# Moving a 64-byte offset from the low parts to the high parts of split weights

## The chip, the cores and the metric

The kernel runs on one core of one Trainium2 chip, in one launch. The metric is the device time of that launch in microseconds. The engines named below are TensorE (PE in the profile, its weight loads PEld), VectorE (DVE), ScalarE (ACT), GpSimd (POOL) and the sync engine (SP), which issues most of the DMAs.

## The reference

The reference is one decoder layer over 256 tokens and a model width of 2048, all in float32:

```python
proj = x @ w_in                      # 13,336 columns: gq gk gv gr glr fq fk fv ff ma mb
y_gla = (rms(gla(q, k, v, log_a)) * g * silu(gr)) @ w_branch_gla
y_fox = fox_attention(fq, fk, fv, log_f) @ w_branch_fox
x = layer_norm(ALPHA * x + (sigmoid(ma) * y_gla + sigmoid(mb) * y_fox) @ w_out)
h = gelu(causal_dwconv(x @ w_gate, conv_w, conv_b)) * (x @ w_up)     # width 5632
x = layer_norm(ALPHA * x + h @ w_down)
x = x + sigmoid(x @ w_ple_gate) * (p @ w_ple_proj)
```

Nearly all of the work is the products of the 256 rows of `x` with some 400 MB of weights.

## The kernel before, in words

**Split products.** A float32 product is made of three products of the type float32r, which the kernel uses as a shorter float32. Each operand is split into a high part (`hi`, a copy into float32r, on ACT) and a low part (`lo = raw - hi`, on DVE). The product is then high by high, high by low and low by high. An activation tile (`xT`, `x1T`, `x2T`) holds, for each of its four blocks of 128 rows of the contraction, 256 high columns (the tokens) and after them 256 low columns.

**Units.** The weights are cut into 284 units of 128 partitions by 2048 columns, in the order in which they are used. `prep()` prepares the next unit: two DMAs fill two tiles `raw` (1024 columns each), ACT writes the two tiles `hi`, DVE the two tiles `lo`. `prep_s()` does the same for units that are multiplied by Strassen's scheme, with the inner function `split()`. `unit()` keeps about three units ahead. The tiles `hi` come from the pool `rhi` and the tiles `lo` from the pool `rlo`, six buffers each, which are used in turn. In `rhi` a buffer has 1024 columns of 4 bytes (4,096 bytes in each partition), in `rlo` 1152 columns (4,608 bytes), of which 1024 are used. Both steps are multiples of 512 bytes.

**Two ways to multiply.** The units 32 to 135 and 224 to 283 (`UA`) have moving weights: 128 columns of an activation are loaded into TensorE, and 512 columns of `hi` or `lo` stream past (`x_mm`, `q_unit`, `s_half`; the tiles `psm`, `psa`, `psb`, `gv`, `gr`, `wo`, `dn`, `pg`). The units 0 to 31 (the queries and keys of both mixers) and 136 to 223 (gate and up projection) have stationary weights: 128 columns of the weights are loaded, and the activations stream past. `w_unit` issues 16 pairs of matmuls for each of these units, into the tiles `psfq`, `psfk`, `psq`, `psk`, `psg` and `psu`. The first of a pair (L307, called the long one below) has 128 columns of `hi` as its stationary operand and streams 512 columns, the high and the low half of the activation. The second (L309, the short one) has 128 columns of `lo` and streams the 256 high columns alone. The first three units of the gate and up stage are multiplied in two phases by `w_phase`: there the `hi` matmuls (L322) stream 256 columns too, half of the tokens, as do the `lo` matmuls (L326).

**Offsets.** `lo_tile(u, name)` gives the tile for a low part. For a unit of `UA` the low part begins at the start of its buffer; for a unit with stationary weights it begins `LO_SHIFT` = 16 columns, 64 bytes, into it. High parts begin at the start of their buffers everywhere.

**Order.** SP's queue and parts of PE's are written out by hand; elsewhere the order is that of the program, moved by priorities. A weight load (LDWEIGHTS) is made by the compiler for each matmul.

Of the kernel before, what the change touches and what calls it, by code (L numbers as in the profile page):

```python
# [10 lines left out]
F32R = mybir.dt.float32r  # L11
# [8 lines left out]
P = 128  # L20
# [15 lines left out]
GAPS = (96, 64, 80)  # L36


LO_SHIFT = 16
UA = (range(32, 136), range(224, 284))  # L40
P_STAT = 5000
P_LN1 = (4000, 2000)
# [36 lines left out]
def tile_block(ctx: ExitStack, tc: tile.TileContext, wu, wfv, wpp, xT_in, x_in, pT_in, wlr,  # L79
# [11 lines left out]
    rhi = ctx.enter_context(tc.tile_pool(name="rhi", bufs=6))  # L91
    rlo = ctx.enter_context(tc.tile_pool(name="rlo", bufs=6))
# [12 lines left out]
    def s8(shape, dt=F32, name=None):  # L105
        return big.tile(shape, dt, tag="S8", name=name)

    def t1(name):
        return sm.tile([P, 256], F32, tag="t1", bufs=6, name=name)
# [10 lines left out]
    def copy(o, i, scale=1.0):  # L120
        return nc.scalar.activation(o, i, AF.Copy, bias=0.0, scale=scale)  # L121
# [29 lines left out]
    hS = {}  # L151

    def lo_tile(u, name):
        o = 0 if any(u in r for r in UA) else LO_SHIFT
        return rlo.tile([P, 1152], F32R, tag="lo", name=f"lo{name}")[:, o:o + 1024]

    def differences(r0, r1, h, pinned=False):
        b12, b11, b22, b21 = r0[:, 0:512], r0[:, 512:1024], r1[:, 0:512], r1[:, 512:1024]
        sub = lambda o, a, b: nc.vector.tensor_tensor(o, a, b, ALU.subtract)  # L159
        if h == 0:  # L160
            i = sub(b11, b12, b11)
            if pinned:
                tc.keep_in_program_order(i)
            sub(b12, b12, b22)
        else:
            sub(b22, b22, b11)
            sub(b21, b21, b22)
# [17 lines left out]
    def prep_s(u):  # L185


        r0, r1 = [ring.tile([P, 1024], F32, tag="raw", bufs=5, name=f"raw{u}_{h}")
                  for h in range(2)]
        b12, b11, b22, b21 = r0[:, 0:512], r0[:, 512:1024], r1[:, 0:512], r1[:, 512:1024]  # L190
        rt = (r0, r1)
        if u in parked:
            nc.sync.dma_start(b11, wu[u, :, 512:1024])
            nc.sync.dma_start(r1, wu[u, :, 1024:2048])
            w = s8([P, 2048], name=f"td{u}")
            nc.sync.dma_start(w, td[parked[u]])
            rt = (w[:, 0:1024], w[:, 1024:2048])
        else:
            for h, r in enumerate((r0, r1)):
                nc.sync.dma_start(r, wu[u, :, h * 1024:(h + 1) * 1024])  # L200
        if dn0 <= u < dn0 + NF:
            nh = (u - dn0) // (NF // 2)
            pair = DN_ORDER[nh][(u - dn0) % (NF // 2)]
            i = DN_S[0].index(pair)
            if i % 2 == 0:
                two = s8([P, 8, 256], F32R, name=f"hS{nh}_{pair}")
                nc.sync.dma_start(two.bitcast(F32), sd[i // 2].rearrange(
                    "p (i n) -> p i n", i=8))
                hS[nh, pair], hS[nh, DN_S[0][i + 1]] = two[:, 0:4], two[:, 4:8]

        def split(src, name, e=slice(0, 1024)):
            hi = rhi.tile([P, 1024], F32R, tag="hi", name=f"hi{u}_{name}")[:, e]
            lo = lo_tile(u, f"{u}_{name}")[:, e]
            copy(hi, src)
            nc.vector.tensor_tensor(lo, src, hi.bitcast(F32), ALU.subtract)  # L215
            return [(hi[:, o:o + 512], lo[:, o:o + 512]) for o in range(0, src.shape[1], 512)]

        x11, = split(b11, "b11", slice(512, 1024))
        x22, x21 = split(r1, "b2")
        if u not in parked:  # L220
            differences(r0, r1, 0)
        t3, t1_ = split(rt[0], "t13")
        if u not in parked:
            differences(r0, r1, 1)
        t2_, t4 = split(rt[1], "t24")
        ready[u] = [x11, x21, x22, t1_, t3, t2_, t4]

    def prep(pinned=False):
        u = n_prep[0]
        n_prep[0] += 1  # L230
        if u in s_units:
            prep_s(u)
            return
        his, los = [], []
        for h in range(2):
            raw = ring.tile([P, 1024], F32, tag="raw", bufs=5, name=f"raw{u}_{h}")
            nc.sync.dma_start(raw, wu[u, :, h * 1024:(h + 1) * 1024])
            hi = rhi.tile([P, 1024], F32R, tag="hi", name=f"hi{u}_{h}")
            copy(hi, raw)
            lo = lo_tile(u, f"{u}_{h}")  # L240
            i = nc.vector.tensor_tensor(lo, raw, hi.bitcast(F32), ALU.subtract)  # L241
            if pinned:
                tc.keep_in_program_order(i)
            his.append(hi)
            los.append(lo)
        ready[u] = (his, los)


    def unit(ahead=3):
        u = n_used[0]  # L250
        n_used[0] += 1
        while n_prep[0] < min(NU, u + ahead):
            prep()
        return ready.pop(u)
# [203 lines left out]
    for u in range(8):  # L458
        hi, lo = fvu[u]
        for j in range(2):  # L460
# [8 lines left out]
            for t, i, c in seq:  # L469
                o, n = fch[c]  # L470
# [14 lines left out]
        elif u == 4:  # L485
            load_consts()
    prep()
    prep()
    wraw = s8([GROWS, 1024], name="wraw")
    nc.gpsimd.memset(wraw, 0.0)  # L490
# [161 lines left out]
    for n in range(16):  # L652
        h, j = n // 2, n % 2
        hi, lo = unit()
# [114 lines left out]
    for n in range(16):  # L769
        nm, dst, sc = (("q", gq, 1.0 / 16.0), ("k", gk, 1.0))[n // 2 % 2]  # L770
        h, c = n // 4, n % 2
        hi, lo = unit()
# [647 lines left out]
    for n in range(NF):  # L1420
# [18 lines left out]
        u = t1("up")  # L1439
# [4 lines left out]
        if pair in DN_S[0]:  # L1444
            if j == 0:
                yp = t2("yp").rearrange("p (k t) -> p k t", t=S)
            h = yp[:, j, :]
        else:
            h = y
# [4 lines left out]
        if pair in DN_S[0] and j == 1:  # L1454
            v = s_sums(yp)
            for i in range(2):
# [5 lines left out]
                o = k % 2 * 1024 + 512 * i  # L1462
# [295 lines left out]
```

## Time and profile before

| | |
|---|---|
| median of 3 runs | 1645.13 us (1644.68 to 1645.78) |
| the profiled execution | span 1645.0 us from the first to the last instruction |
| TensorE | 1638.4 us, 8422 matmuls; weight loads 1404.3 us |
| VectorE, ScalarE, GpSimd | 1356.0 us, 910.3 us, 92.7 us |
| granted TensorE clock | 1.000 |
| from HBM | 417.53 MB, 290 GB/s over the span |

TensorE has a matmul in work all the time, so a matmul's recorded duration overlaps the next one's. What counts is the distance from one start to the next. The view of the chain of waits merges matmuls that follow each other without a gap, with the time of the whole stretch and their number: a stretch divided by its number is that distance.

### The profile page before, as it was taken

What the parts mean: (1) busy time and instruction counts of PE and PEld (TensorE: products, weight loads), DVE (VectorE), ACT (ScalarE), POOL (GpSimd) and SP (SyncE); (2) the same over time, 40 slices, a digit from 0 to 9 for tenths busy, and PEclk for the clock granted to TensorE, in tenths of its full rate; (3) what the DMA queues carried; (4) which work ended last, traced back from release to release, by engine and by line L of the source; (5) the groups of instructions that cost most, each with busy time, mean ns of one, the idle gap of its engine ahead of it and who ended that gap; (6) DMA issues with size and microseconds to landing.
All of it is one profiled execution on the core that took longest, in us unless ns stands there. A gap on an engine that the chain in (4) does not pass through costs nothing.

```text
span 1645.0 us, 23490 instructions
## 1 busy us (share of the span) xinstructions
PE 1638.4 (100%) x8422; PEld 1404.3 (85%) x8422; DVE 1356.0 (82%) x1964; ACT 910.3 (55%) x1277; POOL 92.7 (6%) x244
## 2 busy tenths in 40 slices
PE   9999999999999999999999999999999999999998
PEld 9988888888888888887898888888888888888887
DVE  7687899788989867778987888887887778988887
ACT  6655555456666654446574445555455456566554
POOL 0000000000000000000010111110111000000000
PEclk9999999999999999999999999999999999999999
DMA  8799799878888768889855898888766679899574
GB/s 324 281 371 341 290 383 356 294 258 309 306 333 307 252 207 303 305 335 364 296 190 194 315 338 320 308 306 304 279 239 217 210 260 336 305 343 348 177 258 157
DMA packets 114838, 477.81 MB, mean 290 GB/s; under 512 B 13032, under 2 KB 14320, under 8 KB 95136
## 3 DMA queue, kind: packets, MB, share of 16 engines
q1 hardware_dynamic: 105216, 417.57, 70.8%
q0 software_dynamic: 9504, 58.73, 8.9%
q8 instruction: 66, 1.08, 0.2%
q14 instruction: 52, 0.43, 0.1%
HBM read 417.53 MB, written 58.73 MB: 290 GB/s over the span
## 4 chain that ended last, share of the span: by engine, by line
PE 97%; DMA 1%; DVE 1%; ACT 0%; issue 0%; POOL 0%; ACTq 0%
PE psm L979 11%; PE dn L841 10%; PE psu L307 10%; PE psg L307 9%; PE psa L979 5%; PE psu L309 5%; PE psg L309 5%; PE dn_p L841 4%; PE gr L841 3%; PE gv L841 3%; PE fv L472 3%; PE pg L353 3%; PE psb L979 3%; PE wo L841 2%; PE gr_p L841 2%; PE gv_p L841 2%
## 5 line engine op out<-in xcount | busy, mean ns | idle before, releaser
L241 DVE TENSOR_TENSOR lo<-raw,hi 128x1024 fp32r<-128x1024 f32 x456 | 551.1, 1220 | 140.7 <-ACT hi L121 139.4
L121 ACT ACTIVATE hi<-raw 128x1024 fp32r<-128x1024 f32 x456 | 476.6, 1057 | 304.2 <-DMA raw<-in_wu_dram 83.7
L307 PE MATMUL psu<-x1T,hi 128*128 128x512 f32 x688 | 240.4, 392 | 0.0
L307 PE MATMUL psg<-x1T,hi 128*128 128x512 f32 x672 | 234.8, 392 | 0.0
L309 PE MATMUL psu<-x1T,lo 128*128 128x256 f32 x688 | 192.3, 280 | 0.0
L309 PE MATMUL psg<-x1T,lo 128*128 128x256 f32 x672 | 187.8, 280 | 0.0
L979 PE MATMUL psm<-hi,xT 128*128 128x512 f32 x512 | 163.0, 392 | 0.0
L307 PEld LDWEIGHTS psu<-x1T,hi 128*128 128x128 f32 x688 | 129.2, 188 | 27.6
L307 PEld LDWEIGHTS psg<-x1T,hi 128*128 128x128 f32 x672 | 126.2, 188 | 27.0
L309 PEld LDWEIGHTS psu<-x1T,lo 128*128 128x128 f32 x688 | 130.6, 190 | 0.0
L121 ACT ACTIVATE hi_b<-raw 128x512 fp32r<-128x512 f32 x112 | 92.9, 841 | 66.8 <-DMA raw<-in_wu_dram 17.9
L309 PEld LDWEIGHTS psg<-x1T,lo 128*128 128x128 f32 x672 | 127.6, 190 | 0.0
L159 DVE TENSOR_TENSOR td<-td 128x512 f32<-128x512 f32 x172 | 117.6, 684 | 0.9
L215 DVE TENSOR_TENSOR lo_b<-raw,hi_b 128x512 fp32r<-128x512 f32 x112 | 104.9, 952 | 15.9 <-ACT hi_b L121 15.6
L979 PEld LDWEIGHTS psm<-hi,xT 128*128 128x128 f32 x512 | 96.2, 188 | 19.6
L215 DVE TENSOR_TENSOR lo_t<-td,hi_t 128x1024 fp32r<-128x1024 f32 x86 | 101.7, 1219 | 12.7 <-ACT hi_t L121 12.0
L121 ACT ACTIVATE hi_t<-td 128x1024 fp32r<-128x1024 f32 x86 | 88.0, 1053 | 28.9 <-DMA td<-td 15.1
L979 PE MATMUL psm<-lo,xT 128*128 128x512 f32 x256 | 99.8, 390 | 0.0
L841 PE MATMUL dn<-hi,hC 128*128 128x512 f32 x352 | 97.8, 389 | 0.0
L979 PE MATMUL psa<-hi,oT 128*128 128x512 f32 x256 | 81.2, 392 | 0.0
L841 PEld LDWEIGHTS dn<-hi,hC 128*128 128x128 f32 x352 | 66.0, 188 | 13.7
L979 PEld LDWEIGHTS psa<-hi,oT 128*128 128x128 f32 x256 | 48.1, 188 | 10.0
(414 smaller groups left out, 3130.8 us busy)
## 6 DMA issues: line engine op xcount, KB each, us to landing
raw<-in_wu_dram SPq DMA_DIRECT2D x525, 512.0 KB, 6.3
td<-in_wu_dram SPq DMA_DIRECT2D x43, 1024.0 KB, 8.8
td<-td POOLq DMA_DIRECT2D x43, 1024.0 KB, 7.7
td<-td SPq DMA_DIRECT2D x43, 1024.0 KB, 8.3
hS<-sd SPq DMA_DIRECT2D x11, 1024.0 KB, 8.8
raw<-in_wu_dram SPq DMA_DIRECT2D x43, 256.0 KB, 7.7
fvraw<-in_wfv_dram SPq DMA_DIRECT2D x13, 524.0 KB, 6.6
sd<-hs POOLq DMA_DIRECT2D x24, 256.0 KB, 5.6
```

What stands on the lines that cost most here:

```text
L121: return nc.scalar.activation(o, i, AF.Copy, bias=0.0, scale=scale)
L159: sub = lambda o, a, b: nc.vector.tensor_tensor(o, a, b, ALU.subtract)
L215: nc.vector.tensor_tensor(lo, src, hi.bitcast(F32), ALU.subtract)
L241: i = nc.vector.tensor_tensor(lo, raw, hi.bitcast(F32), ALU.subtract)
L307: nc.tensor.matmul(ps, lhsT=hi[i // 8 if hoff == 0 else 0][:, w0 % 1024:w0 % 1024 + P], rhs=a[:, kt % 4, :], start=first and i == 0, stop= ...
L309: nc.tensor.matmul(ps[:, 256:512], lhsT=lo[i // 8 if hoff == 0 else 0][:, w0 % 1024:w0 % 1024 + P], rhs=a[:, kt % 4, 0:256], start=False, ...
L353: nc.tensor.matmul(bs[j][:, 0:m], lhsT=x, rhs=v[:, o:o + m], start=first and i == 0, stop=last and i == 2)
L472: nc.tensor.matmul(fbk[t][c][:, 0:n], lhsT=x, rhs=w[:, o:o + n], start=kt == 0 and i == 0, stop=kt == 15 and i == 2)
L841: nc.tensor.matmul(ps[:, e], lhsT=x, rhs=w, start=k == 1, stop=k == total.get(id(ps), 3 * ns))
L979: nc.tensor.matmul(ps[t], lhsT=x, rhs=v, start=first and i == 0 and j == 0, stop=last and i == 3 and j == 2)
```

## The change

In units with stationary weights the high parts now begin 64 bytes into their buffers and the low parts at the start. In units of `UA` both begin at the start, as before. The spare columns go with it: a buffer of `rhi` has 1152 columns now, a buffer of `rlo` 1024. The two pools together keep their size, so all tiles behind them stay where they are. No instruction is added, removed or put in another place.

```diff
-LO_SHIFT = 16
+HI_SHIFT = 16
...
     def lo_tile(u, name):
-        o = 0 if any(u in r for r in UA) else LO_SHIFT
-        return rlo.tile([P, 1152], F32R, tag="lo", name=f"lo{name}")[:, o:o + 1024]
+        return rlo.tile([P, 1024], F32R, tag="lo", name=f"lo{name}")
+
+    def hi_tile(u, name):
+        o = 0 if any(u in r for r in UA) else HI_SHIFT
+        return rhi.tile([P, 1152], F32R, tag="hi", name=f"hi{name}")[:, o:o + 1024]
...
         def split(src, name, e=slice(0, 1024)):
-            hi = rhi.tile([P, 1024], F32R, tag="hi", name=f"hi{u}_{name}")[:, e]
+            hi = hi_tile(u, f"{u}_{name}")[:, e]
             lo = lo_tile(u, f"{u}_{name}")[:, e]
...
-            hi = rhi.tile([P, 1024], F32R, tag="hi", name=f"hi{u}_{h}")
+            hi = hi_tile(u, f"{u}_{h}")
             copy(hi, raw)
             lo = lo_tile(u, f"{u}_{h}")
```

## The prediction

> **What bounds the kernel now.** I read the page first: the busy times, the chain that ended last, then who waited for whom on TensorE.
>
> ```profile
> span 1645.0 us, 23490 instructions
> PE 1638.4 (100%) x8422; PEld 1404.3 (85%) x8422; DVE 1356.0 (82%) x1964; ACT 910.3 (55%) x1277; POOL 92.7 (6%) x244
> PE 97%; DMA 1%; DVE 1%; ACT 0%; issue 0%; POOL 0%; ACTq 0%
> ```
>
> ```profile
> PE warm_ps L131 <- DVE warm L128: 1.2, 1, 1.2
> PE wo L841 <- DVE lo_b L215: 0.4, 1, 0.4
> PE wo_p L841 <- ACT hi_t L121: 0.2, 1, 0.2
> ```
>
> TensorE is the bound from end to end: 97% of the chain is matmuls, and the waits of TensorE for other engines come to 1.8 us, none of them at a unit with stationary weights. What the change can move is therefore the distance between matmuls. The groups of the units with stationary weights come next, which are the only units where an address within 512 bytes changes (columns: busy us, mean ns of one, then the engine's idle us before them).
>
> ```profile
> L307 PE MATMUL psu<-x1T,hi 128*128 128x512 f32 x688 | 240.4, 392 | 0.0
> L307 PE MATMUL psg<-x1T,hi 128*128 128x512 f32 x672 | 234.8, 392 | 0.0
> L309 PE MATMUL psu<-x1T,lo 128*128 128x256 f32 x688 | 192.3, 280 | 0.0
> ...
> L309 PEld LDWEIGHTS psu<-x1T,lo 128*128 128x128 f32 x688 | 130.6, 190 | 0.0
> L307 PEld LDWEIGHTS psu<-x1T,hi 128*128 128x128 f32 x688 | 129.2, 188 | 27.6
> ...
> L309 PE MATMUL psfq<-xT,lo 128*128 128x256 f32 x128 | 35.9, 280 | 0.0
> L309 PE MATMUL psk<-xT,lo 128*128 128x256 f32 x128 | 35.8, 280 | 0.0
> ```
>
> These are 688 pairs for `psu`, 672 for `psg` and four times 128 for the queries and keys (two of the four rows): 1,872 pairs. The loads differ by the part: 188 ns for `hi`, 190 ns for the shifted `lo`. Before a load of `hi` the load port is idle (27.6 us over 688 loads, 40 ns each), before a load of `lo` never. The timeline of a piece of the gate and up stage shows why: matmuls first, then the loads in the same place.
>
> ```profile
> 1000.15 0.28 PE L309 MATMUL psg<-x1T,lo 128*128 128x256 f32 x1
> 1000.27 0.39 PE L307 MATMUL psg<-x1T,hi 128*128 128x512 f32 x1
> 1000.50 0.28 PE L309 MATMUL psg<-x1T,lo 128*128 128x256 f32 x1
> ```
>
> ```profile
> 1000.16 0.19 PEld L307 LDWEIGHTS psg<-x1T,hi 128*128 128x128 f32 x1
> 1000.27 0.19 PEld L309 LDWEIGHTS psg<-x1T,lo 128*128 128x128 f32 x1
> ```
>
> A load starts with the matmul ahead of its own. So `hi` is loaded under a short matmul: load at 1000.16, its matmul already at 1000.27, about 0.07 us before the recorded end of the load (the record has that much of a tail). And `lo` is loaded under a long matmul: load at 1000.27, its matmul at 1000.50, 0.04 us after the end of the load. The load under the long matmul has about 110 ns to spare, the load under the short one none that shows here. The change exchanges which of them is the shifted one. The chain of waits gives the distances without rounding.
>
> ```profile
> 900.25 0.23 PE psg L307
> ...
> 904.41 0.23 PE psg L307
> ```
>
> ```profile
> 627.02 10.88 PE psb L979 x48
> ...
> 542.84 2.09 PE go L1084 x9
> ...
> 834.26 1.44 PE psg L322 x12
> ...
> 1638.07 1.20 PE pg_11c L909 x10
> ```
>
> Twelve pairs lie between the first two rows: 4.16 us, 346.7 ns for a pair. Matmuls of 512 columns with an unshifted load under each (`psb`, moving weights) stand 10.88/48 = 226.7 ns apart, those of 256 columns (`psg` at L322, `pg_11c`) 1.44/12 = 1.20/10 = 120.0 ns. The sum of the two is 346.7 ns. So a pair costs today just what its matmuls cost alone with unshifted loads: the shift of `lo`, under the long matmul, costs nothing. `go` is a chain of 512 columns that is slower: 2.09/9 = 232.2 ns, 5.5 ns more for each, without an idle moment. Its operands are no weights: `vh` and `vl` come from a pool that lies behind tiles of a few bytes each, so most of its streams start at another place within 512 bytes. I take it for the size of what an address can cost.
>
> **The change part by part.** *Units with moving weights.* The new buffers stand 4,608 bytes apart for `hi` and 4,096 for `lo`, and `rlo` begins 6 x 512 bytes later, all multiples of 512. Within 512 bytes nothing moves. `psb`'s stretch above mixes `hi` and `lo`, whose buffers stand 4,096 and 4,608 apart today, in one even step. Cost: zero.
>
> *Writing the parts.* ACT now writes `hi` 64 bytes on in the 240 tiles of stationary units, DVE reads it there and writes `lo` at the start. First the gate and up stage (900 to 1320 us, shifted `lo`), then the down projection (1340 to 1540, unshifted), for DVE and for ACT:
>
> ```profile
> L241 DVE TENSOR_TENSOR lo<-raw,hi x152: 1206/1218/1228, 899.1 to 1311.1; 128x1024 fp32r<-128x1024 f32 x152
> ```
>
> ```profile
> L241 DVE TENSOR_TENSOR lo<-raw,hi x38: 1204/1218/1227, 1351.6 to 1531.5; 128x1024 fp32r<-128x1024 f32 x38
> ```
>
> ```profile
> L121 ACT ACTIVATE hi<-raw x151: 1038/1060/1071, 899.9 to 1310.0; 128x1024 fp32r<-128x1024 f32 x151
> ```
>
> DVE's median is 1218 ns with and without the shift. No row has ACT writing a shifted tile; the nearest is DVE's, no difference, and ACT's own spread, 33 ns, bounds it at 240 x 33 ns = 7.9 us of ACT's time in either direction. The cover is that TensorE waits 1.8 us in all for others: cost zero. Without that cover it would be at most those 7.9 us.
>
> *The load of `lo` under the long matmul* becomes unshifted. It had 110 ns to spare, and `psb` shows 226.7 ns for a long matmul over an unshifted load: no gain and no loss.
>
> *The load of `hi` under the short matmul* becomes shifted, 1,872 times. This is the one term. What a shift does to a load stands in the answers by tile (minimum, median, maximum in ns):
>
> ```profile
> L307 PEld LDWEIGHTS psu<-x1T,hi x688: 187/188/188, 849.3 to 1320.5; 128*128 128x128 f32 x172
> ...
> L309 PEld LDWEIGHTS psu<-x1T,lo x688: 187/188/192, 849.5 to 1320.6; 128*128 128x128 f32 x172
> ```
>
> ```profile
> L909 PEld LDWEIGHTS pg_11b<-hi,x2T x12: 188/192/192, 1635.5 to 1637.7; 128*128 128x128 f32 x12
> ```
>
> Under the pairs of `psu`, unshifted loads never exceed 188 ns; shifted ones reach 192, and with the mean of 190 about half of them do. In `pg_11b`, where every matmul is short and every load unshifted, a load is recorded with 192 ns at a step of 120: there the step and the load are as long as each other, and nothing is left for a longer load. I take the mean difference, 190 - 188 = 2 ns, as the growth of the pair, since it is measured on the same kind of tile at the same rate: 1,872 x 2 ns = 3.7 us. Bounds: above, what a bad address costs the `go` chain, 5.5 ns, with these 2 ns on top, 7.5 ns x 1,872 = 14.0 us; below zero too, by the rows of the second rival, -3.6 ns x 1,872 = -6.7 us.
>
> The Trainium skill speaks against this term: its page "TensorE: Matmul & The Clock Gate", section "LDWEIGHTS (loading the stationary operand)", gives a load's time from its number of columns alone, whatever the address, and by it the term is zero. The rows disagree in the small: 188 and 190 ns for the same 128 columns.
>
> *Sum.* The profiled execution's span is 1645.0 us, 0.1 us from the median of 1645.13, so the difference goes on the median: 1645.1 + 3.7 = 1648.9 us (0.23% more).
>
> **The rivals.** *No change.* Today the short matmul is followed by the next one a little early: in the timeline above 0.12 us, and the pair is still 346.7 ns. If a longer load only uses up that, and the stream of columns stays the bound, a pair stays at 226.7 + 120.0 and the time at 1645.1 us. For it: the sum agrees with today's pair to 0.1 ns although one of its loads reaches 192 ns. Against it: `go`, where an address alone costs 5.5 ns a matmul. The Trainium skill gives the same result by its page "SBUF — State Buffer", section "Who interferes with whom": TensorE's two read ports, for the streamed operand and for the loads, are independent and wait for nobody. `go` at 232.2 ns against 226.7 does not bear that out fully.
>
> *Faster.* The short matmul may gain by a shifted load. In the second phase of `w_phase` all matmuls are short and every second load, that of `lo`, is shifted:
>
> ```profile
> 838.35 0.28 PE L322 MATMUL psu<-x1T,hi 128*128 128x256 f32 x1
> ...
> 840.95 0.28 PE L322 MATMUL psg<-x1T,hi 128*128 128x256 f32 x1
> ```
>
> Eleven pairs in 2.60 us are 236.4 ns a pair, against 240.0 for two unshifted ones: 3.6 ns less. If that is the shifted load's doing, and it holds under a contiguous stream, 1,872 pairs give back 6.7 us: 1638.4 us. For it: it is the only place where a shifted load lies under a short matmul. Against it: the streams there are two pieces of 128 columns with a gap, and today's pairs, which have one shifted load each, gain nothing. It decides where the stream and not the load sets the step.
>
> *Slower by more.* If the shifted load and the stream of the short matmul meet as in `go`, each pair grows by 5.5 ns and more: 1645.1 + 10.3 = 1655.4 us, up to 1659.1 with the upper bound. It is the first case at another price, and shares its chance.
>
> *The change does nothing it says.* The offset could be lost if `unit()` handed out the whole buffer; but `hi_tile` returns the cut tile, as `lo_tile` does today. I give it no chance of its own.
>
> **How the numbers follow.** What a measurement of this kernel can tell from no change is about 0.2%, 3.3 us. The term of the load, from 2 to 7.5 ns a pair, is always above this: 0.50, and the likeliest; its own range is 1648.4 to 1659.1 us. No change: 0.22. Faster by the stream: 0.28, since it has a direct row but under another stream. The range from 1638.4 to 1659.1 takes in the bounds of all three and leaves out what would touch both matmuls of a pair.
>
> **What would show it.** In the changed profile the load rows of L307 should read about 190 ns (up to 192) and those of L309 188 ns; the chain's pair in the gate and up stage about 348.7 ns instead of 346.7; `psb` and `dn` as before at 226.7 ns; DVE's L241 at 1218 ns and ACT's L121 at 1060 ns. The forecast is wrong if the pair stands at 346.7 with the 192 ns loads now under the short matmul (no change), if it falls to some 343 ns (the stream gains), or if the time moves while the pair doesn't, which would put it into the preparing engines or the moving weights.

## The result and the profile after

| | before | after |
|---|---|---|
| median of five executions | 1645.19 us | 1654.47 us |
| lowest and highest | 1644.68 to 1646.85 | 1650.61 to 1655.39 |
| the profiled execution | span 1645.0 us | 1655.15 us, span 1653.4 us |

The changed kernel is slower by 9.3 us; the ratio of the times is 1.0051, with an interval from 1.0039 to 1.0063. Line numbers are higher by three in the changed kernel: the long matmul of a pair is L310, the short one L312. First the page's head and busy times, then who waited for whom on TensorE (total us, times, longest).

```profile
span 1653.4 us, 23490 instructions
PE 1647.3 (100%) x8422; PEld 1405.3 (85%) x8422; DVE 1356.4 (82%) x1964; ACT 910.4 (55%) x1277; POOL 93.7 (6%) x244
```

```profile
PE warm_ps L131 <- DVE warm L128: 1.2, 1, 1.2
PE fv L475 <- ACT fvhi L121: 0.2, 1, 0.2
```

The number of instructions is the same, the waits for other engines come to 1.4 us, and the busy times of DVE, ACT and the loads have moved by 1 us or less. TensorE alone is busy for 8.9 us more. The chain of waits shows where (start in us, duration, engine, tile, line); the two rows are twelve pairs apart, in the gate and up stage.

```profile
1000.02 0.23 PE psu L310
...
1004.26 0.23 PE psg L310
```

Twelve pairs take 4.24 us, 353.3 ns for each, where they took 4.16 us, 346.7 ns. Over 85 units of 16 pairs that is 85 x 16 x 6.67 ns = 9.1 us, the whole loss. The answer for the tile `psu` bounds the stage from the other side: the first load starts at 848.5 us and the last at 1328.7, so the stage lasts 480.2 us; in the profile before it went from 849.3 to 1320.5, 471.2 us. The difference is 9.0 us.

```profile
L310 PEld LDWEIGHTS psu<-x1T,hi x688: 187/188/188, 848.5 to 1328.7; 128*128 128x128 f32 x172
L312 PEld LDWEIGHTS psu<-x1T,lo x688: 187/188/188, 848.6 to 1328.8; 128*128 128x128 f32 x172
```

The same rows (minimum, median, maximum) tell that no load became longer. The shifted `hi` takes 188 ns at most, and so does `lo`. The groups of the page agree (busy us, mean ns | idle us before them):

```profile
L310 PE MATMUL psu<-x1T,hi 128*128 128x512 f32 x688 | 244.8, 396 | 0.0
L312 PE MATMUL psu<-x1T,lo 128*128 128x256 f32 x688 | 193.2, 281 | 0.0
L310 PEld LDWEIGHTS psu<-x1T,hi 128*128 128x128 f32 x688 | 129.0, 188 | 31.7
L312 PEld LDWEIGHTS psu<-x1T,lo 128*128 128x128 f32 x688 | 129.1, 188 | 0.0
```

The 190 ns of the shifted `lo` are gone, nothing has them now, and yet it is the matmuls that grew: the long one from 392 to 396 ns, the short one from 280 to 281.

In the queries and keys the chain shows two different steps for the same addresses, in two units of one execution: twelve pairs in 4.20 us (350.0 ns) and in 4.08 us (340.0 ns).

```profile
159.90 0.23 PE psq L310
...
164.10 0.23 PE psk L310
```

```profile
200.02 0.23 PE psk L310
...
204.10 0.23 PE psq L310
```

Added over the trace, the distances in these four tiles together come to 0.5 us more than before: most units stand at 350.0, 3.3 ns above the 346.7 of before, and units 9, 21, 22 and 24 at 340.0, 6.7 ns below it, with parts of their neighbours. The two nearly cancel. What was to stay as it was has stayed: two answers by line for the gate and up stage (DVE and ACT, with the median 1218 and 1060 ns before) and two stretches of moving weights from the chain.

```profile
L244 DVE TENSOR_TENSOR lo<-raw,hi x154: 1206/1219/1229, 896.4 to 1319.1; 128x1024 fp32r<-128x1024 f32 x154
```

```profile
L121 ACT ACTIVATE hi<-raw x154: 1040/1060/1069, 894.3 to 1318.0; 128x1024 fp32r<-128x1024 f32 x154
```

```profile
627.90 10.88 PE psb L982 x48
...
1349.09 6.12 PE dn L844 x27
```

10.88/48 = 6.12/27 = 226.7 ns, as before.

### The profile page after: what moved, and what is told of

Its sections match the earlier page's. It is cut to its first block, busy times and chain, and to the rows that moved or that the text cites. A ratio compares the mean times of both kernels' runs of the same rounds, so it can differ in the third digit from the quotient of the medians.

```text
span 1653.4 us, 23490 instructions
## 1 busy us (share of the span) xinstructions
PE 1647.3 (100%) x8422; PEld 1405.3 (85%) x8422; DVE 1356.4 (82%) x1964; ACT 910.4 (55%) x1277; POOL 93.7 (6%) x244
## 4 chain that ended last, share of the span: by engine, by line
PE 98%; DMA 1%; DVE 0%; ACT 0%; POOL 0%; SPq 0%; issue 0%; ACTq 0%; POOLq 0%
PE psm L982 11%; PE dn L844 10%; PE psu L310 10%; PE psg L310 10%; PE psa L982 5%; PE psu L312 5%; PE psg L312 5%; PE dn_p L844 4%; PE wo L844 3%; PE gr L844 3%; PE gv L844 3%; PE pg L356 3%; PE psb L982 3%; PE fv L475 2%; PE gr_p L844 2%; PE gv_p L844 2%
## 5 line engine op out<-in xcount | busy, mean ns | idle before, releaser
L310 PE MATMUL psu<-x1T,hi 128*128 128x512 f32 x688 | 244.8, 396 | 0.0
L310 PE MATMUL psg<-x1T,hi 128*128 128x512 f32 x672 | 239.1, 396 | 0.0
L312 PE MATMUL psu<-x1T,lo 128*128 128x256 f32 x688 | 193.2, 281 | 0.0
L312 PE MATMUL psg<-x1T,lo 128*128 128x256 f32 x672 | 188.7, 281 | 0.0
L310 PEld LDWEIGHTS psu<-x1T,hi 128*128 128x128 f32 x688 | 129.0, 188 | 31.7
L310 PEld LDWEIGHTS psg<-x1T,hi 128*128 128x128 f32 x672 | 126.0, 188 | 30.9
L312 PEld LDWEIGHTS psu<-x1T,lo 128*128 128x128 f32 x688 | 129.1, 188 | 0.0
L312 PEld LDWEIGHTS psg<-x1T,lo 128*128 128x128 f32 x672 | 126.2, 188 | 0.0
L218 DVE TENSOR_TENSOR lo_t<-td,hi_t 128x1024 fp32r<-128x1024 f32 x86 | 101.6, 1219 | 12.5 <-ACT hi_t L121 12.0
```

The costliest lines, as they stand in the source:

```text
L310: nc.tensor.matmul(ps, lhsT=hi[i // 8 if hoff == 0 else 0][:, w0 % 1024:w0 % 1024 + P], rhs=a[:, kt % 4, :], start=first and i == 0, stop= ...
L312: nc.tensor.matmul(ps[:, 256:512], lhsT=lo[i // 8 if hoff == 0 else 0][:, w0 % 1024:w0 % 1024 + P], rhs=a[:, kt % 4, 0:256], start=False, ...
```

## The experiments

Two theories were set against each other. **The load theory** is that of the prediction: a shifted part takes longer to load, and what it costs depends on the matmul under which it is loaded. **The theory of settled steps** came from the two steps above: a pair falls into one of a few steps, the offsets of `hi` and `lo` decide which ones are open to it, and a step once taken is kept until something else comes between the pairs on TensorE. The times behind the first table are device times as there; the comparison is always with the kernel before on the same chip. Where steps of single units are told, they are distances of the long matmuls' starts in the trace, averaged over whole repetitions of their pattern in the later half of a unit. A step is an average: at 353.3 the pairs of the changed kernel alternate between 350 and 357 ns, and a step of 340.0 has 340 ns for each pair.

**No shift at all** (e1_none). From the changed kernel:

```diff
-HI_SHIFT = 16
+HI_SHIFT = 0
```

> Both parts at the start of their buffers in all units. Load theory (a load of a shifted part is itself longer, and that counts only under the short matmul): no load is shifted, a pair takes 346.7 ns in both stages, 1645 us like the kernel before. State theory (load and stream of a pair settle, after each interruption, into one of a few steps, about 340.0, 346.7, 350.0 or 353.3 ns a pair, and the offsets decide which of them there are): the pair may stand at any of these; if the shift of the low parts is what holds the kernel before at 346.7, pairs of 350 to 353 ns appear here too, and the time is 1650 to 1658 us.

Measured: 1655.23 us (1654.73 to 1656.53), before 1645.07, ratio 1.0064 [1.0047, 1.0081]. The chain in the gate and up stage and the load of `lo`:

```profile
1000.11 0.23 PE psu L310
...
1004.35 0.23 PE psg L310
```

```profile
L312 PEld LDWEIGHTS psu<-x1T,lo 128*128 128x128 f32 x688 | 130.0, 189 | 0.0
```

Again 4.24 us, 353.3 ns a pair, in all 85 units. With neither part shifted the kernel is as slow as the changed one. So the 9 us do not need a shifted `hi`; the shift of `lo` had kept the kernel before from them, and the change gave that up. The load theory, which expected the time before, falls here. The pattern within the step is another one (349, 350 and 361 ns in turn), with the same average.

**Interruptions between units** (e2_kick_after, e3_kick_before). To the changed kernel and to the kernel before, ahead of every fourth unit of gate and up, one to four transposes into a spare PSUM tile that nobody reads:

```diff
     def gate_up(name):
...
+        if n_used[0] % 4 == 3:
+            kp = mxtile("kick")
+            for i in range(1 + n_used[0] // 4 % 4):
+                nc.tensor.transpose(kp[:, i * P:i * P + P], ident, ident)
         hi, lo = unit()
```

> The changed kernel, with one to four extra 128-column transposes on TensorE before every fourth unit of the gate and up stage (some 21 interruptions of 0.1 to 0.5 us, 5 to 8 us in all, results unused). Load theory: every unit keeps its 353.3 ns a pair, since the addresses are the same. State theory: the interruptions draw the state anew, and some groups of four units run at 340.0 or 350.0 ns a pair, others at 353.3, with the same addresses.

> The same interruptions in the kernel before. Both theories: 346.7 ns a pair in all units. The state theory says so because the kernel before came back to 346.7 after every interruption of the queries and keys; a group at another step would mean that it has more than one state too.

Measured in one execution each: 1655.61 us after, 1651.13 us before. The changed kernel takes three steps. The chain has two of them here, 4.08 us for twelve pairs (340.0 ns) and 4.24 us (353.3); the third is 350.0.

```profile
895.21 0.23 PE psu L310
...
899.29 0.23 PE psu L310
...
962.88 0.23 PE psu L310
...
967.12 0.23 PE psg L310
```

Units 147 to 154 stand at 340.0, 159 to 162 and 167 to 170 at 353.3, nearly all others at 350.0; the step changes behind transposes and never between them. The kernel before stays at 346.7 in each of its 85 units, whatever interrupts it:

```profile
1000.05 0.23 PE psg L307
...
1004.21 0.23 PE psg L307
```

So with `lo` at 64 bytes only one step shows; with `hi` at 64 bytes there are three, and the uninterrupted kernel had drawn the slowest of them at the start of the stage and kept it.

**All offsets in turn** (e4_scan_lo, e5_scan_hi). Transposes ahead of every second unit, and from unit 139 on another offset for every eleven units, in steps of 64 bytes; of `lo` in the kernel before, of `hi` in the changed one. The other part lies at 0. The totals, 1661.24 and 1661.57 us, contain the transposes and are not compared.

```diff
         o = 0 if any(u in r for r in UA) else LO_SHIFT
+        if 139 <= u < 224:
+            o = 16 * ((u - 139) // 11)
```

> The kernel before, with low parts 0, 64, 128, ... 448 bytes into their buffers, in eight groups of 11 units of the gate and up stage (the last has 8), high parts at the start, and one to four extra 128-column transposes before every second unit. Load theory: 346.7 ns a pair at every offset, because the shifted load lies under the long matmul with 110 ns to spare. State theory: the offset sets which steps there are, so groups differ, some with several steps among their units; the group at 64 bytes stays at 346.7.

> The kernel after with one to four transposes ahead of every second gate/up unit and with hi at another offset in every eleven units from 139 on (0, 64, 128, ... 448 bytes), lo at 0 throughout. Load theory (the load of a shifted hi lasts longer): the load takes 188 ns at 0 and about 190 at every other offset, and the pair follows it. Theory of settled steps (a pair falls into one of a few steps, and the addresses decide which ones are open to it): the load stays at 188 ns at every offset, steps of 340.0, 346.7, 350.0 and 353.3 ns appear, the same set at offsets 256 bytes apart; at 64 and 320 bytes 340.0, 350.0 or 353.3, never the steady 346.7 that a lo at 64 gives.

Steps seen, in ns a pair (one execution of each kernel, eleven units at an offset, eight at 448):

| offset | `lo` moved, `hi` at 0 | `hi` moved, `lo` at 0 |
|---|---|---|
| 0, 256 | 346.7, 353.3 | 346.7, 353.3 |
| 64, 320 | 346.7 only | 340.0, 350.0, 353.3 |
| 128, 384 | 346.7, 350.0 | 352.0 |
| 192, 448 | 346.7, 350.0 | 340.0, 350.0 |

(At 64 the units with `hi` moved showed only 350.0 and 353.3 in this run, at 320 all three; at 448 the units with `lo` moved showed 350.0 alone.) Four readings from the chains: first `lo` at 64 (eight pairs in 2.77 us) and at 128 (eight in 2.80 us), then `hi` at 128 (ten in 3.52 us) and at 192 (eight in 2.72 us). At 128 the pairs of `hi` repeat a pattern of five distances between 346 and 359 ns, so only five or ten of them give the average, 352.0.

```profile
948.74 0.23 PE psg L309
...
951.51 0.23 PE psg L309
...
989.06 0.23 PE psu L309
...
991.86 0.23 PE psu L309
```

```profile
1005.45 0.24 PE psg L312
...
1008.97 0.24 PE psg L312
...
1046.57 0.23 PE psu L312
...
1049.29 0.23 PE psu L312
```

As far as these few units show it, the table repeats with 256 bytes. With neither part shifted, at 0, both 346.7 and 353.3 occur: the 353.3 of e1 is one of two steps there. The 352.0 was in neither expectation. Over all offsets together the load of `hi` has a median of 188 ns, with 192 at most:

```profile
L312 PEld LDWEIGHTS psu<-x1T,hi x688: 187/188/192, 848.7 to 1335.3; 128*128 128x128 f32 x172
```

The load theory expected one step at 0 and another at all other offsets. The chain has up to three steps at one offset, and the one offset pair of `lo`, 64 and 320 bytes, at which only 346.7 is ever seen is the one that the kernel before uses.

**Can the step be chosen?** (e6_kick8_after, e8_once5, e9_once6, e10_seq_two, e11_seq_five). The step of 340.0 is faster than anything before, so it was tried to reach it in the changed kernel. First one to eight transposes ahead of every unit:

```diff
+        kp = mxtile("kick")
+        for i in range(1 + n_used[0] % 8):
+            nc.tensor.transpose(kp[:, i % 4 * P:i % 4 * P + P], ident, ident)
         hi, lo = unit()
```

> The kernel after with one to eight transposes ahead of each gate/up unit. Load theory: every unit at one step (the same load under the same matmul), 353.3 ns a pair. Theory of settled steps: the units part into 340.0, 350.0 and 353.3 ns a pair, with the load at 188 ns in all of them; if the number of transposes decides which, units with the same number agree. The transposes themselves add about 85 x 4.5 x 0.07 = 27 us or more.

Measured, in one execution: 1690.36 us, of which the transposes are some 35 us. From unit 148 to 223 the steps repeat with the eight units: behind five transposes 353.3, behind six 340.0, seven 350.0, eight 340.0, one to four 350.0. The same counts had other results in e2 (two transposes kept 340.0 there), so the count alone doesn't decide. Then a few transposes only at the start of the stage, after which nothing else comes:

```diff
+        if n_used[0] == 140:
+            kp = mxtile("kick")
+            for i in range(5):
```

> The kernel after with five transposes ahead of gate/up unit 140 and nothing else added. Theory of settled steps: the units before it run at 353.3 ns a pair; after five transposes the earlier run with transposes ahead of every unit went from 353.3 to 340.0, and the step stays until PE does something else, so 84 units x 16 pairs x 13.33 ns = 17.9 us go, about 0.5 us of transposes come: 1637 us, 8 us under the kernel before. If it falls on 350.0 instead: 1654.5 - 84 x 16 x 3.33 ns = 1650 us. Load theory, or a theory in which the offset alone sets the step: 1655 us.

> As the run with five, with six transposes, which in the earlier run led from 353.3 to 340.0 as well (units 157, 165, 173 and on). Theory of settled steps: 340.0 from unit 140 on, 1637 us; 1650 us at 350.0, 1655 us at 353.3. Load theory: 1655 us.

```diff
+        if 139 <= n_used[0] <= 140:
+            kp = mxtile("kick")
+            for i in range(n_used[0] - 135):
```

> The kernel after with four transposes ahead of gate/up unit 139 and five ahead of unit 140, as the run with transposes ahead of every unit began, and none behind. Theory of settled steps: unit 139 at 353.3 ns a pair, then 340.0 from unit 140 to 223, since nothing else interrupts: 1654.5 - 84 x 16 x 13.33 ns = 1636.6, plus about 0.8 us of transposes: 1637.4 us, 8 us under the kernel before; 1651 us where the units fall on 350.0. Load theory: 1655 us in any case.

> The same with four to eight transposes ahead of units 139 to 143, the first five of that run word for word (353.3, 340.0, 353.3, 350.0, 340.0). Theory of settled steps: 340.0 from unit 143 to 223: 1654.5 - 81 x 16 x 13.33 ns = 1637.2, plus 30 transposes or 2.7 us: 1640 us; 1652 us at 350.0. Load theory: 1657 us.

| | median, us | all executions, us | ratio to before |
|---|---|---|---|
| five, once | 1650.65 | eight from 1648.3 to 1651.5; 1641.84; 1638.92 | 1.0018 [1.0001, 1.0035] |
| six, once | 1652.13 | five from 1651.34 to 1652.21 | 1.0036 [1.0022, 1.0050] |
| four, five | 1639.02 | seven from 1637.59 to 1639.26; 1649.95, 1649.99, 1652.63 | 0.9978 [0.9954, 1.0001] |
| four to eight | 1647.20 | five from 1640.65 to 1642.55; five from 1651.86 to 1656.19 | 1.0014 [0.9991, 1.0038] |

With five or six transposes once, the profiled executions stand at 350.0 from unit 140 to the end. The 340.0 and 1637 us that were expected first did not come; the times are near those named for 350.0 (1650 us). So the count and the step before do not decide together either: in e6, five transposes (unit 140) and six (unit 157) led from 353.3 to 340.0, here both led from 353.3 to 350.0. The two short executions with five have times as at 340.0; their steps weren't seen. With four to eight ahead of units 139 to 143, the profiled execution stands at 340.0 from 143 on: first the chain with five transposes (4.20 us for twelve pairs), then that with four to eight (4.08 us).

```profile
1000.27 0.23 PE psg L310
...
1004.47 0.23 PE psg L310
```

```profile
1000.03 0.23 PE psg L310
...
1004.11 0.23 PE psg L310
```

Its time of 1640.65 us is the 1640 expected; five of its ten executions lie near the 1652 named for 350.0 instead. So the same pairs at the same addresses run at 350.0 or at 340.0, after what came once near the start of the stage. But the step is not held for sure. The profiled execution of the kernel with four and five transposes is one of its three long ones, and shows how it is lost. It runs at 340.0 up to unit 155, as the first two rows of the chain show; then, from the timelines, a load of `lo` waits for DVE and DVE for ACT; from there on the chain stands at 350.0.

```profile
899.83 0.23 PE psg L310
...
903.91 0.23 PE psg L310
```

```profile
943.47 0.19 PEld L312 LDWEIGHTS psg<-x1T,lo 128*128 128x128 f32 x1 [0.21 <-DVE lo L244]
```

```profile
942.19 3.50 DVE L244 TENSOR_TENSOR lo<-raw,hi 128x1024 fp32r<-128x1024 f32 x3 [1.50 <-ACT hi L121]
```

```profile
959.96 0.23 PE psg L310
...
964.16 0.23 PE psu L310
```

The wait itself costs 0.2 us. The slower step in which the pairs stand behind it, for the remaining 68 units, costs 68 x 16 x 10 ns = 10.9 us, about the 11 to 14 us between the two groups of times in the table. Whether the other long executions have the same cause wasn't seen. Nor does every such wait change the step. In the profiled execution with five transposes once, the same load of unit 156 waits longer, 0.30 us, and the pairs stay at 350.0 (in e7 below, 0.6 us at this unit leave 346.7 as it was):

```profile
944.23 0.19 PEld L312 LDWEIGHTS psg<-x1T,lo 128*128 128x128 f32 x1 [0.30 <-DVE lo L244]
```

The version with four and five transposes has the lowest median of all, 6.5 us under the kernel before, but the interval of its ratio just reaches 1, so that it beats the kernel before is likely and not shown.

**Where the shift of `lo` matters** (e7_lo_gu). The kernel before with the shift in gate and up alone:

```diff
-        o = 0 if any(u in r for r in UA) else LO_SHIFT
+        o = 0 if u < 136 or any(u in r for r in UA) else LO_SHIFT
```

> The kernel before with the shift of lo in gate/up alone (units 136 to 223); in units 0 to 31 both parts lie at the beginning. Theory of settled steps: gate/up runs at 346.7 ns a pair as in the kernel before, queries/keys as in the kernel without a shift (346.7 mostly, a few units at 353.5): 1645 to 1647 us. Theory that both stages carry the loss (spread evenly over the 1,872 pairs): 1645 + 512/1872 x 10 = 1648 us.

Measured: 1646.08 us, ratio 1.0003 [0.9993, 1.0012]. Gate and up stays at 346.7 throughout. In queries and keys a few units fall to 353.3, like this one, the others stay at 346.7:

```profile
90.51 0.23 PE psfq L307
...
94.75 0.23 PE psfk L307
```

There TensorE does other work between units, and the step changes (units 7 to 11 and 26 stand at about 353, with parts of their neighbours); in gate and up nothing comes between, and one step holds for 85 units. So the shift of `lo` in gate and up is enough to keep the time of before.

**Distance or place** (e12_both_64). The kernel before, with transposes ahead of every second gate and up unit, and both pools moved 64 bytes on:

```diff
-GAPS = (96, 64, 80)
+GAPS = (112, 48, 80)
```

> The kernel before (lo 64 bytes behind hi) with both pools moved 64 bytes on against everything else, and one to four transposes ahead of every second gate/up unit; hi now lies 64 bytes and lo 128 bytes into the 512, the streamed activations where they were. Units with moving weights move too, so the total is not compared, only the pairs of gate/up. Theory that the distance between the two stationary parts decides: 346.7 ns a pair in every unit, as before. Theory that the place of hi and lo decides, each by itself or against the streamed activations: steps as with hi at 64 bytes, 340.0, 350.0 or 353.3, or steps not seen yet. Load theory: 346.7 everywhere with 190 ns for the loads of both.

Measured, in one execution: 1671.17 us. The chain of gate and up, then two stretches of moving weights:

```profile
906.56 0.23 PE psg L307
...
910.76 0.23 PE psg L307
```

```profile
632.02 10.99 PE psb L979 x48
```

```profile
1352.51 6.18 PE dn L841 x27
```

Twelve pairs in 4.20 us: 350.0 ns, in all units but two at 353.3. The distance between `lo` and `hi` is still 64 bytes, and the steady 346.7 is gone. So the distance of the two parts alone doesn't decide; where they lie does. Whether that counts by itself or against the streamed activations, which stayed in place, is open. Moving weights feel it as well: 10.99/48 = 229.0 ns and 6.18/27 = 228.9 instead of 226.7.

## Why the prediction was right and wrong

The direction was right, and the time of 1654.5 us lies in the range, 5.6 us above the forecast of 1648.9. The mechanism was not what the prediction said, and that the time fell into the range is luck: at the same addresses gate and up can also run at 350.0 or 340.0 ns a pair, and at 340.0 the time would be about 1654.5 - 85 x 16 x 13.33 ns = 1636.4 us, faster than before and below the range.

**What held.** The bound: only distances between matmuls moved. The costs set to zero: DVE's write took 1219 ns (1218 before), ACT's 1060 (1060), moving weights 226.7 ns. That nothing moves within 512 bytes for moving weights carried more than the prediction knew: e12 shows what 64 bytes would have cost there.

**The step that failed first** is "So a pair costs today just what its matmuls cost alone with unshifted loads: the shift of `lo`, under the long matmul, costs nothing." The sum of 226.7 and 120.0 was put together from chains of equal matmuls; no pair of a long and a short matmul with both loads unshifted stood in the trace. Measured, such a pair takes 353.3 ns in the whole stage of e1, and 346.7 or 353.3 in the scans with both parts at 0. So 346.7 was one step out of two and no fixed cost of the matmuls, and the shift of `lo` not only cost nothing: it held the pair at the faster of the two, 6.7 ns below e1.

**From it the second error:** "The load of `lo` under the long matmul becomes unshifted ... no gain and no loss". That is the part of the change that brings the loss. Without the shift of `lo`, and with `hi` unshifted too, e1 is as slow as the changed kernel.

**The one term of the sum,** "the load of `hi` under the short matmul becomes shifted", 2 ns on each of 1,872 pairs, does not exist: the load stayed at 188 ns. A load recorded at 190 or 192 ns does not mark a slower pair; the kernel before has them at 346.7 and the changed one lacks them at 353.3. Nor does it mark a shifted one: the prediction's own row of `pg_11b` has 192 ns with every load unshifted, and in the scan of `hi` the mean load of `lo`, which stayed at 0, went from 187.8 to 189.7 ns. On this the Trainium skill was right, which the prediction weighed and set aside: its page "TensorE: Matmul & The Clock Gate", section "LDWEIGHTS (loading the stationary operand)", gives a load's time by its number of columns, with no term for the address, and the rows agree to within 2 ns (medians of 187 to 190 ns for the moved part at every offset of the scans). Two smaller points of the sum change nothing: the bound of 1648.4 us is the 0.2% of noise and not the 2 ns, which give 1648.9; and the span of 1645.0 us and the median of 1645.13 are different measures (after, the profiled execution has a span of 1653.4 and a time of 1655.15 us).

**The rivals.** *Slower by more* gave 5.5 to 7.5 ns a pair and 1655.4 to 1659.1 us; the 6.7 ns and 1654.5 us are close to it, but over 1,360 pairs instead of 1,872 and not by a meeting of the shifted load with the stream. *Faster* expected some 343 ns; a faster step, 340.0, does exist, also at other offsets of `hi`, but only a few units of queries and keys fell into it. The row that it rested on does depend on the shift: with no part shifted (e1), eight pairs of two short matmuls take 1.92 us, 240.0 ns each, where the kernel before had 236.4.

```profile
838.32 0.12 PE psg L325
...
840.24 0.12 PE psu L325
```

The gain did not carry over to pairs with a long matmul. *No change* failed in gate and up. The rule that it cited (the Trainium skill, "SBUF — State Buffer", "Who interferes with whom": the two read ports of TensorE wait for nobody) would, taken that way, give one step at all offsets; the scans have 340.0 to 353.3. That leaves open which of the reads, or what else, waits.

**Not settled:** what makes a step at given addresses, and which of the open steps an interruption leads to. Neither the count of transposes nor the count with the step before settles it (e2, e6, e8, e9), and executions of one kernel on one chip came out differently (e8, e10, e11). One execution of the changed kernel took 1650.61 us, which 350.0 ns in gate and up instead of 353.3 would give (1654.5 - 85 x 16 x 3.33 ns = 1650.0 us); its steps weren't seen.

## What to carry to other kernels

When a chain of matmuls with alternating shapes is the bound, compare the distance of two starts with the fastest one that the trace ever shows for this pattern, not with a sum taken from other patterns: a steady step without any wait can still be a slow one. Offsets of operands in SBUF are worth a scan with an interruption now and then, which shows more of the steps that an offset allows, where a plain run shows only the one that it happened to fall into. An offset with one good step can be worth more than one with a better step that a late operand can end.

## What the runs showed of the hardware

A pair of a 512-column and a 256-column matmul with a load under each runs at 340.0, 346.7, 350.0, 352.0 or 353.3 ns on average, with the same instructions, loads recorded with 187 to 192 ns and a granted clock of 0.999 or 1.0. Which of these can occur depends on where the stationary operands lie within 256 bytes; which of them does occur depends on what TensorE did before, and it then lasts, up to 85 units or 1,360 pairs without a change. One wait of 0.21 us went with its end (340.0 to 350.0, e10); waits of 0.30 and 0.6 us left 350.0 (e8) and 346.7 (e7) as they were. Streams of weights moved by 64 bytes against the loaded activations stand 229.0 ns apart instead of 226.7 (e12).
